# The first two weight tiles behind a sub-layer border: 258-column products of both tiles ahead of the 256-column ones

## The chip, the cores and the metric

The kernel runs as one program on 1 core of one Trainium2 chip. The metric is device time in microseconds (us) of one execution; lower is better. Three runs of the kernel before gave 945.15, 945.64 and 947.23 us, median 945.64 us.

## The reference

Two decoder layers over 256 tokens and 1024 features, all in float32. Each layer is FFN, token mixer, FFN; the mixer is stick-breaking attention in layer 0 and a gated linear recurrence (RG-LRU) in layer 1. Every sub-layer first normalises its input and modulates it with a shift, a scale and a gate that come from a conditioning vector:

```python
def sublayer_input(x, g, mod_j):
    shift, scale, gate = mod_j[:, 0], mod_j[:, 1], mod_j[:, 2]
    h = rmsnorm(x, g) * (1 + scale[:, None, :]) + shift[:, None, :]
    return h, (1 + gate)[:, None, :]
...
for layer in range(DEPTH):
    h, g = sublayer_input(x, norm_g[layer, 0], mod[:, 0])
    x = x + MACARON_W * g * swiglu(h, ffn_w_gu[layer, 0], ffn_w_down[layer, 0])
    h, g = sublayer_input(x, norm_g[layer, 1], mod[:, 1])
    if layer % N_MIXERS == 0:
        y = stick_breaking_attention(h, sb_w_qkv[j], sb_w_o[j])
    else:
        y = rglru_block(h, lru_w_in[j], lru_conv_w[j], lru_conv_b[j], lru_w_r[j], lru_b_r[j],
                        lru_w_i[j], lru_b_i[j], lru_lambda[j], lru_w_out[j])
    x = x + g * y
    h, g = sublayer_input(x, norm_g[layer, 2], mod[:, 2])
    x = x + MACARON_W * g * swiglu(h, ffn_w_gu[layer, 1], ffn_w_down[layer, 1])
return rmsnorm(x, final_norm_g)
```

So there are six sub-layers, and five borders between one sub-layer and the next.

## The kernel before, in words

The activations lie transposed: a chunk is 128 features (partitions) by T = 256 tokens (columns), eight chunks (KD) make one activation. A weight tile is 128 output features of two kinds (two halves, `g` = 0 and 1, of 128 columns each) by eight chunks of input features.

**Three products for one.** A float32 product is made from three products in the type fp32r. Weights and activations are each split into a high part, rounded to fp32r, and a low part, what the rounding left. `group` (the matmul stands in line 615) issues for each chunk and half up to three passes: pass 0 is high weight by high activation (`wh` by `xh`), pass 1 is high weight by low activation (`wh` by `xl`), pass 2 is low weight by high activation (`wl` by `xh`). For a weight tile that is 8 chunks x 2 halves x 3 passes = 48 products of 128 x 128 weights by 256 columns. ScalarE (ACT) writes the high weight parts (line 585), VectorE (DVE) the low ones (line 588), in two pieces of 1024 columns for each tile.

**Rings of buffers.** `wh` and `wl` hold seven such pieces each. `hx` holds 20 activation parts, with a pitch of 320 columns; `hk` holds two more. In the built program the ring `hx` begins at byte 102720 of a partition and its pitch is 1280 bytes, so that all its buffers begin 64 bytes behind a multiple of 256; the two buffers of `hk` begin at bytes 128384 and 129408, 128 behind a multiple of 256, and all pieces of `wh` and `wl`, when they are loaded as weights, also 128 behind one. `hk` holds a copy of chunk 0, high and low (line 763 and `other_copy`), that some of the tiles behind a border use in place of the one in `hx` (`up` with `kick=True`): the six products of chunk 0 then read their columns from `hk`, and the next ones from `hx` again.

**A border.** The last step of a sub-layer (`down`) adds its output to `x` chunk by chunk (line 794). At once `scaled` writes the scaled but not yet normalised chunk, high on ACT and low on DVE (line 730), and ACT copies two columns behind the high part (the shift, high and low), so that it has TX = 258 columns. The first two weight tiles (NFIRST) of the next sub-layer are multiplied with these chunks in `up_first`, and the norm is applied to their results afterwards: 256 columns are scaled with the norm's factor, and columns 257 and 258 are what the shift adds. Of the three passes, 0 and 2 have 258 columns and pass 1 has 256. Between these products TensorE adds up the squares over the partitions (`rstd`, line 705, two products with the weights `none`); ACT makes the norm's factor of the sum, and then DVE and ACT write the normalised chunks (`norm`, lines 738, 557 and 746) for all further tiles. Two tiles take 96 products, and `rstd` two.

**What sets the order.** `Program.schedule` orders all instructions by a planner's cost table while the program is built: TensorE's products mostly as written, ACT's and DVE's by how late the planner thinks they may be. `rstd` is written ahead of the 37th product of the first border (the one to attention) and ahead of the 49th of the others.

The five borders lead to attention, to the second FFN, to layer 1's first FFN, to the RG-LRU and to the last FFN, in this order.

Of the kernel before, what the change touches and what calls it, by code (L numbers as in the profile page):

```python
# [10 lines left out]
AF = mybir.ActivationFunctionType  # L11
ALU = mybir.AluOpType
PSUM = bass.MemoryType.PSUM

P = 128
T = 256
TX = T + 2
D = 1024
KD = D // P
# [11 lines left out]
HALF = 1024  # L31
SQ = 8
NFIRST = 2
LAT0, RATE0, RATE = 1250.0, 404.0, 360.0
LAT1 = 1250.0
LASTY = 900.0
# [357 lines left out]
def c_act(n, psum=False, ptr=0):  # L394
    return (51.0 if psum else 93.0) + 0.8333 * n + 93.0 * ptr


def c_dve(n):
    return 68.0 + 1.042 * n


def c_mm(n, passes=3):
    return (432.0 if passes == 4 else 114.0 * passes) * max(n, 256) / 256
# [7 lines left out]
def trunk(ctx, tc, first_in, cb, par, modw, gu, wdn, qk, wv, wo, win, wri, wout, out):  # L411
# [5 lines left out]
    act, dve, pe, pool, sp = nc.scalar, nc.vector, nc.tensor, nc.gpsimd, nc.sync  # L417
# [6 lines left out]
    def f32(ap):  # L424
        return ap.bitcast(F32)


    def ring(name, n, cols, dt=F32, pl=const, pitch=0):
        if pitch:
            whole = pl.tile([P, n * pitch], dt, tag=name, name=name)  # L430
            tiles = [whole[:, i * pitch : i * pitch + cols] for i in range(n)]
        else:
            tiles = [pl.tile([P, cols], dt, tag=f"{name}{i}", name=f"{name}{i}") for i in range(n)]
        return Space(name, n, lambda at, _: tiles[at]), tiles

    banks, _ = ring("bank", 8, 512, pl=psum)
    banks.exclusive = True
    rawr, _ = ring("raw", 3, CH)
# [14 lines left out]
    hxr, _ = ring("hx", 20, TX, F32R, pitch=320)  # L453
    const.tile([P, HKPAD], F32, tag="pad2", name="pad2")
    hkr, _ = ring("hk", 2, T, F32R)
    sqr, _ = ring("sq", 2, T)
    ssqr, _ = ring("ssq", 2, T)
    rmsr, _ = ring("rms", 1, T)
    rstr, _ = ring("rst", 1, T)
    hpr, _ = ring("hpre", 3, T)  # L460
    bcr, _ = ring("bc", 4, 2)
    tr, _ = ring("tr", 2, T)
    sgr, _ = ring("sg", 3, T)
# [36 lines left out]
    def fixed(name, cols, dt=F32):  # L500
        return const.tile([P, cols], dt, tag=name, name=name)
# [17 lines left out]
    none_ = fixed("none", P, F32R)  # L519
# [35 lines left out]
    def A(o, i, f, n, r, w, table=None, psum=False, ptr=0, after=(), **kw):  # L555
        def fn():
            act.activation(o(), i(), f, **{k: (v() if callable(v) else v) for k, v in kw.items()})  # L557
        return pr.op("ACT", c_act(n, psum, ptr), fn, r, w, after, table)

    def V(fn, n, r, w, cost=None, ptr=0, after=()):  # L560
        return pr.op("DVE", cost or c_dve(n) + 62.0 * ptr, fn, r, w, after)
# [33 lines left out]
    class Acc:  # L595
# [6 lines left out]
        def group(self, part, o, w, wc, xs, xc, stop, parts=(None,), passes=(0, 1, 2), m=None):  # L602

            b = self.b
            start = not self.started
            self.started = True
            wh, wl = w
            xh, xl = xs

            def fn():  # L610
                seq = ((wh, xh), (wh, xl), (wl, xh))
                for n, i in enumerate(passes):
                    u, v = seq[i]
                    c = slice(0, m if i == 1 else None)
                    pe.matmul(o(b())[:, c], wc(u()), xc(v())[:, c], start=start and n == 0,  # L615
                              stop=stop and n == len(passes) - 1, skip_group_check=True)

            n = xs_n[0]
            ws = [wh] * (passes != (2,)) + [wl] * (2 in passes)
            rd = ws + [(xh, q) for q in parts if passes != (1,)] + [(xl, q) for q in parts[:1] if 1 in passes]  # L620
            if not start:
                rd.append((b, "start"))
            wr = [(b, part)] + ([(b, "start")] if start else [])
            return pr.op("PE", c_mm(n, len(passes)), fn, rd, wr)
# [68 lines left out]
    def rstd(gen):  # L693
        qs = ssq.pop(gen)
        b = Buf(banks)
        sign = 1.0
        if not isinstance(qs, tuple):

            t, y, sign = qs, (Buf(hkr), Buf(hkr)), -1.0
            A(y[0], t, AF.Copy, T, [t], [y[0]])  # L700
            V(lambda: dve.tensor_tensor(y[1](), t(), f32(y[0]()), ALU.subtract), T, [t, y[0]], [y[1]])

            def fn():
                for i in range(2):
                    pe.matmul(b()[:, :T], none_, y[i](), start=i == 0, stop=i == 1)  # L705
            pr.op("PE", c_mm(T, 2), fn, list(y), [b])
            qs = ()
        for i, q in enumerate(qs):
            if gen == (0, 0):
                (q, c, h), o = q, slice(0, T)  # L710
            else:
                q, c, h, o = (q[0], q[2], q[1], q[2]) if isinstance(q, tuple) else (q, slice(0, T), None, slice(0, T))
            pr.op("PE", 259.2 if gen == (0, 0) else c_mm(T, 4), lambda i=i, q=q, c=c, o=o: pe.matmul(
                b()[:, o], ones, q()[:, c], start=i == 0, stop=i == len(qs) - 1, skip_group_check=True),
                [(q, h)] + [b] * (i > 0), [b])
        r = Buf(rmsr)
        o = Buf(rstr)
        A(r, lambda: b()[:, :T], AF.Ln, T, [b], [r], table="lnexp", psum=True, ptr=1, bias=eps_t, scale=sign / D)
        A(o, r, AF.Exp, T, [r], [o], table="lnexp", scale=-0.5)
        return o  # L720

    def scaled(gen, d):

        gs, y = mfin[gen + (1,)], shr[gen]
        hi, lo = Buf(hxr), Buf(hxr)
        gcur.setdefault(gen, []).append((hi, lo))
        c = slice(d, d + 1)
        A(lambda: hi()[:, T:], lambda: f32(y()[:, 2 * d : 2 * d + 2]), AF.Copy, 2, [(y, 0), (y, 1)], [(hi, 1)])
        A(lambda: hi()[:, :T], x[d], AF.Copy, T, [x[d], (gs, d)], [(hi, 0)], ptr=1, scale=lambda: gs()[:, c])
        V(lambda: dve.scalar_tensor_tensor(lo()[:, :T], x[d](), gs()[:, c], f32(hi()[:, :T]), ALU.mult, ALU.subtract), T,  # L730
          [x[d], (gs, d), (hi, 0)], [(lo, 0)], ptr=1)
# [19 lines left out]
    def norm(gen, q):  # L751
        for d in range(KD):
            norm_chunk(gen, d, q)
        other_copy(gen)
# [95 lines left out]
    def up_first(gen, ws, scale=(1.0, 1.0)):  # L850


        gx = gcur.pop(gen)
        accs = {}
        for i, w in enumerate(ws):
            accs[i] = [Acc(f"first_{gen}_{i}_{g}") for g in range(2)]
            for k in range(KD):
                if (i, k) == ((0, 6) if gen == (0, 1) else (1, 0)):
                    q = rstd(gen)
                for g in range(2):  # L860
                    c0 = (k % 4) * 256 + g * P
                    group(accs[i][g], 0, lambda b: b[:, :TX], w[k // 4], lambda u, c0=c0: u[:, c0 : c0 + P], gx[k],
                          lambda v: v, TX, k == KD - 1, parts=(0, 1), m=T)

        def evict(i, g):
            b, t, c = accs[i][g].b, Buf(tr), Buf(bcr)
            V(lambda: dve.tensor_scalar(c()[:, :1], b()[:, T : T + 1], b()[:, T + 1 : TX], scale[g], ALU.add, ALU.mult), 1, [b], [c],
              ptr=1, after=[lows[gen]])
            V(lambda: dve.scalar_tensor_tensor(t(), b()[:, :T], scale[g], q(), ALU.mult, ALU.mult), T, [b, q], [t],
              after=[lows[gen]])  # L870
            return t, c, lambda: c()[:, :1]

        norm(gen, q)
        for i in range(len(ws)):
            yield [evict(i, g) for g in range(2)]
# [13 lines left out]
    def ffn(l, s, nxt, hook):  # L889
# [12 lines left out]
        if j == 0:  # L902
            f0 = SQ
            accs = [Acc(f"g0_{f}") for f in range(SQ)]
            first_loads(F)
            q = rstd((0, 0))

            gb, goff, boff = gbias, OFF_NG, OFF_MB
# [92 lines left out]
        else:  # L1001
            f0 = NFIRST

# [17 lines left out]
    def attention(l, s, nxt, hook):  # L1021
# [43 lines left out]
        def q_load(f):  # L1065
            return load(qk[f], CH, f"qk{f}")

        def q_proj(f):
            if f == 0:
                firsts.append(up_first((l, s), [q_load(i) for i in range(NFIRST)], (0.125, 1.0)))  # L1070
            y = qs[f] = Buf(F, 4, name=f"q{f}")
# [4 lines left out]

            if f < NFIRST:
                for g, (t, rd, c) in enumerate(next(firsts[0])):
# [155 lines left out]
    def rglru(l, s, nxt):  # L1234
# [63 lines left out]
        def xb_proj(n2):  # L1298
            if n2 == 0:
                firsts.append(up_first((l, s), [  # L1300
                    load(win[1, i], CH, f"xb{i}", homes=ahead[1, 0] if i == 0 else ()) for i in range(NFIRST)]))
            if n2 < NFIRST:
                ts = next(firsts[0])
# [200 lines left out]
    parts = [(0, 0, 2), (0, 1, 1), (0, 1, 0), (0, 1, 2), (0, 2, 1), (0, 2, 0), (0, 2, 2)]  # L1504
# [96 lines left out]
```

## Time and profile before

| | us |
|---|---|
| median of 3 runs | 945.64 |
| span of the profiled execution | 943.5 |
| PE busy in it | 934.2 |
| DVE busy in it | 780.0 |
| ACT busy in it | 558.3 |
| first border, its 98 products | 193.03 to 204.67 |
| second border | 302.67 to 314.31 |

The profile is that of one execution, on the one core; its span runs from the first to the last instruction, and the median of the runs is 2.1 us above it. Matmuls overlap: a matmul's duration in the profile is longer than the distance from its start to the next one's, so that the pace of TensorE is read from the starts in the timeline, which prints them to 0.01 us, and the count of products between two of them. In the timeline neighbouring instructions of one group share a row, with the start of the first and their number; a product with 256 columns and one with 258 share a row where their tiles are the same.

### The profile page before, as it was taken

The numbers are of one execution on the slowest core, as the hardware profiler recorded it, in microseconds if no ns is written. First come the engines' busy times: TensorE is split into PE (matmuls) and PEld (weight loads), VectorE is DVE, ScalarE is ACT, GpSimd is POOL, SyncE is SP. The second block draws the span as 40 slices with busy tenths as digits, with TensorE's granted clock in tenths as the row PEclk, the third lists the DMA queues.
The fourth block names the chain that finished last, engine by engine and source line by source line (L and its number), as shares of the span: only waits on it lengthen the run. The fifth ranks groups of instructions, "written<-read, shape, count | busy, mean of one in ns | idle before, by whom it ended". The sixth has DMA issues, their size and how long they took to land.

```text
span 943.5 us, 19620 instructions
## 1 busy us (share of the span) xinstructions
PE 934.2 (99%) x8092; PEld 925.7 (98%) x8092; DVE 780.0 (83%) x1247; ACT 558.3 (59%) x921; POOL 2.1 (0%) x14
## 2 busy tenths in 40 slices
PE   8999999999999999999999999999999999999997
PEld 7999999999999999999999999999999999999997
DVE  8999988899978998888899998866999997555444
ACT  6785453488776754454376544535789685544333
POOL 0000000000000000000000000000000000000000
PEclk9999999999999999999999999999999999999999
DMA  9989899958752888889967999886333656555531
GB/s 365 404 335 365 323 345 356 347 207 299 275 202 96 309 335 324 311 328 349 361 263 275 353 336 334 326 332 224 135 129 141 224 184 242 199 184 203 167 118 45
DMA packets 48489, 251.24 MB, mean 266 GB/s; under 512 B 5384, under 2 KB 6288, under 8 KB 28688
## 3 DMA queue, kind: packets, MB, share of 16 engines
q1 hardware_dynamic: 48096, 249.59, 71.2%
q8 instruction: 63, 1.03, 0.4%
q10 hardware_dynamic: 304, 0.40, 0.1%
q14 instruction: 26, 0.21, 0.1%
HBM read 248.92 MB, written 1.05 MB: 265 GB/s over the span
## 4 chain that ended last, share of the span: by engine, by line
PE 95%; DMA 3%; DVE 1%; ACT 0%; SPq 0%; issue 0%; DVEq 0%; ACTq 0%
PE bank L615 89%; DMA raw<-in_first_in 3%; PE bank L1052 2%; PE bank L1285 1%; DMA arenar<-in_first_in 1%; PE bank L1118 1%; PE bank L1179 1%; PE bank L1155 1%; SPq L550 0%; DVE wl L588 0%; ACT wh L585 0%; DVE raw L1416 0%; PE bank L1158 0%; PE bank L1399 0%; PE bank L705 0%; DVE arenar L649 0%
## 5 line engine op out<-in xcount | busy, mean ns | idle before, releaser
L615 PE MATMUL bank<-hx,wh 128*128 128x256 f32 (+1 forms) x3264 | 559.7, 277 | 0.0
L585 ACT ACTIVATE wh<-raw 128x1024 fp32r<-128x1024 f32 (+1 forms) x330 | 336.8, 1038 | 292.7 <-PE bank L615 215.7
L615 PEld LDWEIGHTS bank<-hx,wh 128*128 128x128 f32 x3264 | 493.2, 188 | 0.3 <-DVE hx L951 0.2
L588 DVE TENSOR_TENSOR wl<-raw,wh 128x1024 fp32r<-128x1024 f32 (+1 forms) x330 | 387.7, 1195 | 122.7 <-ACT wh L585 118.7
L615 PE MATMUL bank<-hx,wl 128*128 128x256 f32 (+1 forms) x1640 | 452.5, 277 | 0.2 <-DVE wl L588 0.2
L615 PEld LDWEIGHTS bank<-hx,wl 128*128 128x128 f32 x1640 | 308.1, 188 | 0.4 <-DVE wl L588 0.4
L615 PE MATMUL bank<-arenar,wh 128*128 128x256 f32 x1696 | 289.4, 276 | 0.0
L615 PEld LDWEIGHTS bank<-arenar,wh 128*128 128x128 f32 x1696 | 255.6, 188 | 0.3 <-issue 0.3
L615 PE MATMUL bank<-arenar,wl 128*128 128x256 f32 x848 | 234.2, 276 | 0.0
L649 DVE SCALAR_TENSOR_TENSOR rawm<-rawm,cact 128x1024 f32<-128x1024 f32 x128 | 154.5, 1218 | 7.1 <-DMA rawm<-in_modw 6.8
L615 PEld LDWEIGHTS bank<-arenar,wl 128*128 128x128 f32 x848 | 159.2, 188 | 0.1
L557 ACT ACTIVATE arenar<-a 128x256 fp32r<-128x256 f32 x88 | 35.1, 403 | 7.2 <-DVE a L882 7.1
L887 DVE TENSOR_TENSOR arenar<-a,arenar 128x256 fp32r<-128x256 f32 x88 | 36.2, 417 | 0.5 <-ACT arenar L557 0.5
L882 DVE TENSOR_TENSOR a<-bank,sg 128x256 f32<-128x256 f32 x82 | 34.0, 417 | 0.6 <-ACT sg L557 0.4
L557 ACT ACTIVATE sg<-bank 128x256 f32<-128x256 f32 x82 | 29.8, 367 | 6.7 <-PE bank L615 6.6
L557 ACT ACTIVATE arenaf<-bank 128x256 f32<-128x256 f32 (+1 forms) x53 | 22.8, 486 | 11.9 <-DVE bank L1128 4.5
L794 DVE SCALAR_TENSOR_TENSOR x<-bank,mf,x 128x256 f32<-128x256 f32 (+1 forms) x49 | 21.7, 471 | 9.2 <-PE bank L615 9.1
L557 ACT ACTIVATE hx<-x,mf 128x256 fp32r<-128x256 f32 x40 | 19.1, 499 | 15.7 <-DVE x L794 15.7
L557 ACT ACTIVATE hx<-hpre,mf 128x256 fp32r<-128x256 f32 x41 | 19.9, 500 | 8.7 <-DVE hpre L738 8.6
L1052 PE MATMUL bank<-wh,hx 128*128 128x256 f32 x128 | 23.5, 281 | 0.0
L649 DVE SCALAR_TENSOR_TENSOR arenar<-arenar,cact 128x1024 f32<-128x1024 f32 x16 | 19.4, 1218 | 1.0 <-DMA arenar<-in_first_in 0.9
L1052 PEld LDWEIGHTS bank<-wh,hx 128*128 128x128 f32 x128 | 20.1, 189 | 0.1
(126 smaller groups left out, 504.3 us busy)
## 6 DMA issues: line engine op xcount, KB each, us to landing
raw<-in_gu SPq DMA_DIRECT2D x79, 1024.0 KB, 4.9
rawm<-in_modw SPq DMA_DIRECT2D x128, 512.0 KB, 6.6
raw<-in_wdn SPq DMA_DIRECT2D x44, 1024.0 KB, 5.1
raw<-in_win SPq DMA_DIRECT2D x10, 1024.0 KB, 4.8
arenar<-in_first_in SPq DMA_DIRECT2D x16, 512.0 KB, 8.0
raw<-in_qk SPq DMA_DIRECT2D x8, 1024.0 KB, 5.1
raw<-in_wout SPq DMA_DIRECT2D x5, 1024.0 KB, 5.0
raw<-in_first_in SPq DMA_DIRECT2D x8, 512.0 KB, 8.8
```

Source lines behind the costliest of these rows:

```text
L557: act.activation(o(), i(), f, **{k: (v() if callable(v) else v) for k, v in kw.items()})
L585: act.activation(h()[:, :m], raw()[:, a : a + m], AF.Copy)
L588: dve.tensor_tensor(lo()[:, :m], raw()[:, a : a + m], f32(h()[:, :m]), ALU.subtract)
L615: pe.matmul(o(b())[:, c], wc(u()), xc(v())[:, c], start=start and n == 0, stop=stop and n == len(passes) - 1, skip_group_check=True)
L649: dve.scalar_tensor_tensor(raw(), raw(), 1.0, cact(), ALU.mult, ALU.mult, accum_out=m()[:, t : t + 1])
L794: dve.scalar_tensor_tensor(x[d]()[:, w], acc.b()[:, j * T + w.start : j * T + w.stop], gate()[:, d : d + 1], x[d]()[:, w], ALU.mult, ALU.add)
L882: V(lambda: dve.tensor_tensor(a(), b()[:, T:], sg(), ALU.mult), T, [(b, (1, 0)), sg], [a])
L887: V(lambda: dve.tensor_tensor(y[1](), a(), f32(y[0]()), ALU.subtract), n, [a, y[0]], [y[1]])
L1052: pe.matmul(o, u()[:, tb * P : (tb + 1) * P], v()[:, c0 : c0 + 256], start=start and n == 0, stop=k == KD - 1 and n == 2, skip_group_check ...
L1118: pe.matmul(zb[e][i]()[:, j * m : (j + 1) * m], y()[rows, kc], y()[rows, qc], start=j == 0, stop=j == 1, skip_group_check=True)
L1155: pe.matmul(b()[:, : NC[i]], ntri, blk(q(), i), start=False, stop=i == j == 1, skip_group_check=True)
L1179: pe.matmul(b()[e * 64 : (e + 1) * 64, j * T + tb * P : (j + 1) * T], v()[:, vc : vc + 64], ww[e]()[:, at : at + NC[tb] // 2], start=j == ...
```

## The change

Three things, all in what belongs to a border:

- In `up_first` the order of the 96 products is another one. First come the passes 0 and 2 (258 columns) of tile 0, chunk by chunk, then those of tile 1: 64 products. Then come the passes 1 (256 columns): for each chunk those of tile 0 and of tile 1, 32 products. `rstd` is written ahead of chunk 1 of tile 1 at the first border and ahead of chunk 4 of tile 1 at the others.
- In `scaled` the low parts of chunks 0 and 1 (KICKS) are written to the ring `hk` in place of `hx`. These are the columns of the first 8 of the 32 products of pass 1.
- In `rstd` the two parts of the sum of squares are written to `hx` in place of `hk`.

```diff
+KICKS = 2
...
-            t, y, sign = qs, (Buf(hkr), Buf(hkr)), -1.0
-            A(y[0], t, AF.Copy, T, [t], [y[0]])
-            V(lambda: dve.tensor_tensor(y[1](), t(), f32(y[0]()), ALU.subtract), T, [t, y[0]], [y[1]])
+            t, y, sign = qs, (Buf(hxr), Buf(hxr)), -1.0
+            h, m = lambda: y[0]()[:, :T], lambda: y[1]()[:, :T]
+            A(h, t, AF.Copy, T, [t], [y[0]])
+            V(lambda: dve.tensor_tensor(m(), t(), f32(h()), ALU.subtract), T, [t, y[0]], [y[1]])
...
-                    pe.matmul(b()[:, :T], none_, y[i](), start=i == 0, stop=i == 1)
+                    pe.matmul(b()[:, :T], none_, y[i]()[:, :T], start=i == 0, stop=i == 1)
...
-        hi, lo = Buf(hxr), Buf(hxr)
+        hi, lo = Buf(hxr), Buf(hkr if d < KICKS else hxr)
...
-        accs = {}
-        for i, w in enumerate(ws):
-            accs[i] = [Acc(f"first_{gen}_{i}_{g}") for g in range(2)]
+        accs = [[Acc(f"first_{gen}_{i}_{g}") for g in range(2)] for i in range(len(ws))]
+
+        def products(i, k, passes):
+            for g in range(2):
+                c0 = (k % 4) * 256 + g * P
+                group(accs[i][g], 0, lambda b: b[:, :TX], ws[i][k // 4], lambda u, c0=c0: u[:, c0 : c0 + P], gx[k], lambda v: v,
+                      TX, k == KD - 1 and passes == (1,), parts=(0, 1), passes=passes, m=T)
+
+        for i in range(len(ws)):
             for k in range(KD):
-                if (i, k) == ((0, 6) if gen == (0, 1) else (1, 0)):
+                if (i, k) == ((1, 1) if gen == (0, 1) else (1, 4)):
                     q = rstd(gen)
-                for g in range(2):
-                    c0 = (k % 4) * 256 + g * P
-                    group(accs[i][g], 0, lambda b: b[:, :TX], w[k // 4], lambda u, c0=c0: u[:, c0 : c0 + P], gx[k],
-                          lambda v: v, TX, k == KD - 1, parts=(0, 1), m=T)
+                products(i, k, (0, 2))
+        for k in range(KD):
+            for i in range(len(ws)):
+                products(i, k, (1,))
```

TensorE's order at the second border, its first products, as the kernel before has it. `bank` are the accumulators, `hx` the activation parts, `wh` and `wl` the weight parts (the number behind a name is the buffer); the last column is what the columns' operand is, partitions by columns.

```order
1738 L615 MATMUL bank_67<-arenar_2524,wl_90 128x256
1739 L615 MATMUL bank_65<-hx,wh_84 128x258
1740 L615 MATMUL bank_65<-hx,wh_84 128x256
1741 L615 MATMUL bank_65<-hx,wl_91 128x258
1742 L615 MATMUL bank_70<-hx,wh_84 128x258
1743 L615 MATMUL bank_70<-hx,wh_84 128x256
1744 L615 MATMUL bank_70<-hx,wl_91 128x258
```

The same place with the change; `group`'s matmul is line 616 of the changed file.

```order
1738 L616 MATMUL bank_67<-arenar_2540,wl_90 128x256
1739 L616 MATMUL bank_63<-hx,wh_84 128x258
1740 L616 MATMUL bank_63<-hx,wl_91 128x258
1741 L616 MATMUL bank_70<-hx,wh_84 128x258
1742 L616 MATMUL bank_70<-hx,wl_91 128x258
```

The products with 256 columns have left this place. They stand at the end of the border, opened by eight that read from `hk`:

```order
1803 L616 MATMUL bank_69<-hx,wl_87 128x258
1804 L616 MATMUL bank_63<-hk_95,wh_84 128x256
1805 L616 MATMUL bank_70<-hk_95,wh_84 128x256
1806 L616 MATMUL bank_68<-hk_95,wh_79 128x256
1807 L616 MATMUL bank_69<-hk_95,wh_79 128x256
1808 L616 MATMUL bank_63<-hk_96,wh_84 128x256
1809 L616 MATMUL bank_70<-hk_96,wh_84 128x256
1810 L616 MATMUL bank_68<-hk_96,wh_79 128x256
1811 L616 MATMUL bank_69<-hk_96,wh_79 128x256
1812 L616 MATMUL bank_63<-hx,wh_84 128x256
```

In the kernel before, no product of the border reads `hk` but the two of `rstd`; behind these rows 23 more from `hx` follow, all with `wh`, and then the first tile of the normalised chunks.

ACT's order at the first border, before: `hx<-x` is a scaled high part, `hx<-sh` the two columns of the shift, `wh<-raw` a weight piece of a later tile, `hk<-ssq` the sum of squares for `rstd`.

```order
184 L557 ACTIVATE sq_97<-x 128x256
185 L557 ACTIVATE hx<-sh_186 128x2
186 L557 ACTIVATE hx<-x,mf_158 128x256
187 L557 ACTIVATE lam<-x 128x10
188 L557 ACTIVATE hk_95<-ssq_99 128x256
189 L557 ACTIVATE hx<-sh_186 128x2
190 L585 ACTIVATE wh_84<-raw_73 128x1024
191 L557 ACTIVATE hx<-sh_186 128x2
192 L585 ACTIVATE wh_78<-raw_73 128x1024
```

And with the change:

```order
183 L558 ACTIVATE sq_97<-x 128x256
184 L558 ACTIVATE hx<-x,mf_158 128x256
185 L558 ACTIVATE hx<-sh_186 128x2
186 L586 ACTIVATE wh_84<-raw_73 128x1024
187 L558 ACTIVATE hx<-sh_186 128x2
188 L586 ACTIVATE wh_78<-raw_73 128x1024
189 L558 ACTIVATE hx<-ssq_99 128x256
```

The sum of squares for `rstd` now stands behind these two weight pieces, where it stood ahead of both; the last copy of the shift stands behind one weight piece in either order.

## Prediction

> **What bounds the kernel now.** First the page: the busy times, the clock, the chain that ended last.
>
> ```profile
> span 943.5 us, 19620 instructions
> PE 934.2 (99%) x8092; PEld 925.7 (98%) x8092; DVE 780.0 (83%) x1247; ACT 558.3 (59%) x921; POOL 2.1 (0%) x14
> ...
> PEclk9999999999999999999999999999999999999999
> ...
> PE 95%; DMA 3%; DVE 1%; ACT 0%; SPq 0%; issue 0%; DVEq 0%; ACTq 0%
> ```
>
> TensorE is 95% of the chain and the granted clock is full in all slices. Next, the waits of TensorE:
>
> ```profile
> PE bank L927 <- DVE hpre L743: 1.2, 1, 1.2
> PE bank L1446 <- POOL eps L511: 1.2, 1, 1.2
> PE bank L615 <- DVE wl L588: 0.2, 1, 0.2
> ```
>
> That is 2.6 us in all, none at a border. So a change inside a border can win only by letting TensorE issue the same products at a shorter distance, and lose by making it wait or by lengthening that distance. Hence the timeline, for the distance from start to start. A long stretch behind the second border (groups, then its first and last rows; the row at 423.16 is the first product of the next kind):
>
> ```profile
> L615 PE MATMUL bank<-hx,wh 128*128 128x256 f32 x636 | 108.2, 276 | 0.0
> L615 PE MATMUL bank<-hx,wl 128*128 128x256 f32 x318 | 87.8, 276 | 0.0
> ```
>
> ```profile
> 314.31 0.40 PE L615 MATMUL bank<-hk,wh 128*128 128x256 f32 x2
> ...
> 315.02 0.40 PE L615 MATMUL bank<-hx,wh 128*128 128x256 f32 x2
> ...
> 315.72 0.39 PE L615 MATMUL bank<-hx,wh 128*128 128x256 f32 x2
> ...
> 423.16 0.39 PE L615 MATMUL bank<-arenar,wh 128*128 128x256 f32 x2
> ```
>
> 636 + 318 = 954 products from 315.02 on; the first six take 0.70 us (117 ns each), the other 948 take 107.44 us: **113.3 ns** each. The six from `hk` ahead of them take 0.71 us, 118 ns each. I call 113.3 ns the settled pace. Not every stretch of the same shape has it. Behind the first border, from 204.67 to 216.06:
>
> ```profile
> L1052 PE MATMUL bank<-wh,hx 128*128 128x256 f32 x32 | 6.0, 280 | 0.0
> L615 PE MATMUL bank<-hx,wh 128*128 128x256 f32 x28 | 5.0, 281 | 0.0
> L1052 PE MATMUL bank<-wl,hx 128*128 128x256 f32 x16 | 4.5, 280 | 0.0
> L615 PE MATMUL bank<-hx,wl 128*128 128x256 f32 x14 | 3.9, 281 | 0.0
> L615 PE MATMUL bank<-hk,wh 128*128 128x256 f32 x4 | 0.8, 282 | 0.0
> L615 PE MATMUL bank<-hk,wl 128*128 128x256 f32 x2 | 0.6, 283 | 0.0
> ```
>
> ```profile
> 204.67 0.28 PE L1052 MATMUL bank<-wh,hx 128*128 128x256 f32 x1
> ...
> 209.62 0.40 PE L615 MATMUL bank<-hk,wh 128*128 128x256 f32 x2
> ...
> 216.06 0.49 PE L1118 MATMUL bank<-arenaf 64*128 64x256 f32 x2
> ```
>
> The first 42 products (to 209.62: 48 of L1052 less the six that stand behind the six of `hk`) take 4.95 us, **117.9 ns** each, the unsettled pace; all 96 take 11.39 us, 118.6 ns each. Same columns, same clock, no wait: the pace has a memory, and what stood ahead decides. Now the second border itself:
>
> ```profile
> L615 PE MATMUL bank<-hx,wh 128*128 128x256 f32 x32 | 9.1, 283 | 0.0
> L615 PE MATMUL bank<-hx,wl 128*128 128x258 f32 x32 | 9.0, 282 | 0.0
> L615 PE MATMUL bank<-hx,wh 128*128 128x258 f32 x32 | 9.0, 280 | 0.0
> ```
>
> ```profile
> 302.67 0.40 PE L615 MATMUL bank<-hx,wh 128*128 128x258 f32 x2
> 302.90 0.28 PE L615 MATMUL bank<-hx,wl 128*128 128x258 f32 x1
> 303.02 0.41 PE L615 MATMUL bank<-hx,wh 128*128 128x258 f32 x2
> ```
>
> It ends at 314.31: these 96 and `rstd`'s two, 98 products in 11.64 us, 118.8 ns each. At the settled pace they would take 11.11 us; so five borders hold at most 5 x 0.53 = 2.7 us, 0.28% of the time. Of that the change can win a part. About 0.2% is what a measurement of this kernel can tell from no change, here 1.9 us.
>
> **The change, part by part.** (1) *The 64 products with 258 columns, now in one row.* No such row exists in the trace. Bounds: the settled pace by columns, 113.3 x 258/256 = 114.2 ns; and 120 ns, the distance of single 258-column products (302.90 to 303.02). I take 117.9 ns, the unsettled pace at 256 columns: TensorE comes to the border from settled products, and the third one in it already takes 0.12 us, so a row with the wider ones more likely stays unsettled than not. 64 x 0.1179 = 7.55 us. (2) *`rstd`'s two*, at 0.12 us 0.24 us, before and after. (3) *The eight from `hk`*: 8 x 0.118 = 0.94 us. (4) *The 24 with 256 columns behind them.* In the rows at 314.31 six products from `hk` came straight out of a border, and then `hx` needed six (0.70 us) to settle. Here eight come out of 258-column products in the same way: 0.70 + 18 x 0.1133 = 2.74 us. If they don't settle: 24 x 0.1179 = 2.83 us.
>
> One border is then 7.55 + 0.24 + 0.94 + 2.74 = 11.47 us, against 11.64: 0.17 us won, **0.85 us in five**. With 114.2 ns for (1) it is 0.41 us and 2.04 us; with 120 ns 0.04 us and 0.2 us; not settling in (4) takes back 5 x 0.09 = 0.45 us.
>
> The rule that speaks against it: the Trainium skill, "TensorE: Matmul & The Clock Gate", section "Wait — 56ns, not 53.3ns?", gives a stream's distance as the columns over 2.4 GHz plus some 2.5 ns that are fixed per matmul, so by it order and address cost nothing and the sum would be 0. The trace disagrees, with 113.3 and 117.9 ns for the same 256 columns.
>
> (5) *Behind the first border* no copy of chunk 0 opens the next tile, and the 96 products above ran unsettled. Left in the settled pace they would save 96 x (118.6 - 113.3) = 0.5 us; but they read other operands at once and change them more often than before, so I take half, **0.25 us**, with bounds of 0 and 0.5. At the other four a tile opened from `hk` follows at once, before and after, which settles the pace from either side; from a settled stretch as here:
>
> ```profile
> 62.42 0.39 PE L615 MATMUL bank<-hk,wh 128*128 128x256 f32 x2
> ...
> 63.13 0.40 PE L615 MATMUL bank<-hx,wh 128*128 128x256 f32 x2
> ...
> 63.83 0.39 PE L615 MATMUL bank<-hx,wh 128*128 128x256 f32 x2
> ```
>
> Again 0.71 us and 0.70 us: nothing won or lost there.
>
> (6) *What TensorE now needs earlier.* The last high chunk is needed after 28 to 30 products instead of 36 to 42, and the weights of tile 1 after 32 instead of 48. At the first border, the tightest, ACT has:
>
> ```profile
> 194.98 0.49 ACT L557 ACTIVATE hx<-x,mf 128x256 fp32r<-128x256 f32 x1
> 195.38 0.20 ACT L557 ACTIVATE lam<-x 128x10 f32<-128x10 f32 x1
> 195.48 0.41 ACT L557 ACTIVATE hk<-ssq 128x256 fp32r<-128x256 f32 x1
> 195.80 0.19 ACT L557 ACTIVATE hx<-sh 128x2 fp32r<-128x2 f32 x1
> 195.89 1.04 ACT L585 ACTIVATE wh<-raw 128x1024 fp32r<-128x1024 f32 x1
> 196.84 0.19 ACT L557 ACTIVATE hx<-sh 128x2 fp32r<-128x2 f32 x1
> ```
>
> ```profile
> 195.92 0.43 DVE L701 TENSOR_TENSOR hk<-ssq,hk 128x256 fp32r<-128x256 f32 x1
> ```
>
> In the new order the last high chunk (194.98, 0.40 to the next start) is followed by a shift (0.09), a weight piece (0.95), the last shift (0.19): ready at 196.61. TensorE comes to it after 30 products, 193.03 + 30 x 0.1179 = 196.57. Then another piece (0.95, from 196.51), and the sum of squares from 197.46: ACT 0.41, DVE 0.43, ready at 198.30; TensorE wants it after 44 products, at 198.22. So both arrive on the brink: **0.15 us lost**, bounds 0 and 0.4. The other four have `rstd` four products later and no such squeeze. (7) *The low parts of chunks 0 and 1 in `hk`* keep the copy of chunk 0 waiting until their products are done, after 70 and 74 products, at 310.92 and 311.39 at the second border. There the two copies start later anyway, so it costs nothing:
>
> ```profile
> 311.19 0.42 ACT L557 ACTIVATE hk<-hx 128x256 fp32r<-128x256 f32 x1
> ```
>
> ```profile
> 311.90 0.29 DVE L763 CAST hk<-hx 128x256 fp32r<-128x256 f32 x1
> ```
>
> DMAs, bytes and the number of instructions stay; no queue is passed by a DMA.
>
> **Sum:** -0.85 - 0.25 + 0.15 = -0.95 us: the profiled execution from 943.5 to 942.5 us, and the median, 2.1 us above it, from 945.64 to **944.7 us**.
>
> **The rivals.**
> - *A row of 258-column products settles* at 114.2 ns. For it: in settled stretches all products of a row have one width, and the border mixes two. Against: at the border's entry the settled pace is lost within three products. 2.04 + 0.25 - 0.15 = 2.1 us won, 943.5 us.
> - *Nothing settles:* the row runs at 120 ns, and the last 24 stay at 117.9. -0.2 + 0.45 + 0.15 = +0.4 us, 946.0 us; with only one of the two, about 945.5 us. For it: eight from `hk`, all with `wh`, is not the pattern of six that the trace shows settling.
> - *The distance depends on the columns alone*: 945.6 us. By the skill's page this is the outcome; with two paces in the rows it has little.
> - *Slower:* the six from `hk` behind a border no longer settle the 948 products after them, because they now come out of another state. One such stretch costs 948 x (117.9 - 113.3) = 4.4 us, so that a single one of the four borders decides: 945.64 - 0.95 + 4.4 = 949.1 us. Against it: rows 314.31 and 62.42 settle from both states.
>
> **How the numbers follow.** Forecast (row of 258 unsettled, 256 settled) 0.50; the row settles 0.22; nothing settles 0.16; columns alone 0.05; slower 0.07. Faster by over 1.9 us needs the row to settle, three in four of these cases (943.5 is only just beyond), 0.165, and a tenth of the forecast's: 0.22. Slower: 0.07. Between: 0.71. The range goes from a settled row with all of (5), 945.64 - 2.4 = 943.2, to 946.0, where nothing settles.
>
> **What would show it.** Right: in the timeline of a border 64 products with 258 columns take 7.4 to 7.7 us, the last 18 with 256 columns 2.04 us, and TensorE has no wait of over 0.4 us there. Wrong: 7.3 us for the 64 (settled, and the gain is double), 0.1179 us each at the end (no settling), a stretch of 948 that lasts 111.8 in place of 107.4 us, or waits for the sum of squares, a shift or a normalised low part at several borders.

## The result, and the profile after

| | median, us | lowest to highest | executions |
|---|---|---|---|
| before | 945.91 | 945.15 to 953.63 | 20 |
| changed | 952.01 | 945.66 to 952.72 | 20 |

The ratio is 1.0048, with a 95% interval of 1.0036 to 1.0061: slower by some 0.5%, where I had forecast 944.7 us and had put the upper end at 946.0. The executions of the changed kernel fall into two groups, which the medians hide: 5 of the 20 lie at 945.7 to 946.9, as before, and 15 at 951.9 to 952.7. I call the second group the long executions. With the later runs below they are 20 of 33; of the kernel before they are 6 of 103.

The profile that came with the result is of a short one (span 944.6, device time 946.28 us). Its page: busy times and the chain as before.

```profile
span 944.6 us, 19604 instructions
PE 934.9 (99%) x8092; PEld 926.3 (98%) x8092; DVE 780.0 (83%) x1247; ACT 558.6 (59%) x921; POOL 2.1 (0%) x14
...
PE 95%; DMA 4%; DVE 0%; ACT 0%; issue 0%; SPq 0%; DVEq 0%; ACTq 0%
```

TensorE's longest waits, of which none is at a border:

```profile
PE bank L935 <- DVE hpre L745: 1.4, 1, 1.4
PE bank L1454 <- POOL eps L512: 1.2, 1, 1.2
```

The second border and the stretch behind it in TensorE's timeline (start, duration, operation, count):

```profile
303.27 0.28 PE L616 MATMUL bank<-hx,wh 128*128 128x258 f32 x1
...
309.07 0.40 PE L707 MATMUL bank<-hx,none 128*128 128x256 f32 x2
309.31 0.28 PE L616 MATMUL bank<-hx,wh 128*128 128x258 f32 x1
...
311.24 0.64 PE L616 MATMUL bank<-hk,wh 128*128 128x256 f32 x4
...
312.20 0.41 PE L616 MATMUL bank<-hx,wh 128*128 128x256 f32 x2
...
314.94 0.39 PE L616 MATMUL bank<-hk,wh 128*128 128x256 f32 x2
...
315.65 0.40 PE L616 MATMUL bank<-hx,wh 128*128 128x256 f32 x2
...
423.84 0.39 PE L616 MATMUL bank<-arenar,wh 128*128 128x256 f32 x2
```

The 64 wide products take 5.80 + 1.93 = 7.73 us, 120.8 ns each; `rstd` 0.24; the eight from `hk` 0.96; the 24 behind them 2.74: together 11.67 us, against 11.64 before. Then six from `hk` in 0.71 and 954 products in 108.19 us, 113.4 each with the first six. So in a short execution the border wins nothing and the stretch is settled. The first border:

```profile
193.64 0.28 PE L616 MATMUL bank<-hx,wh 128*128 128x258 f32 x1
...
205.31 0.28 PE L1060 MATMUL bank<-wh,hx 128*128 128x256 f32 x1
...
216.66 0.49 PE L1126 MATMUL bank<-arenaf 64*128 64x256 f32 x2
```

11.67 us again (before 11.64), and 11.35 us for the 96 products behind it (before 11.39). It begins 0.6 us later than before, which comes from the start of the kernel: in two later profiles of the same program it begins at 194.11 (look_1) and 192.97 us (look_2).

### The profile page after: what moved, and what is told of

The parts are those of the page before. It is cut to its first block, busy times and chain, and to the rows that moved or that the text cites. A ratio compares the mean times of both kernels' runs of the same rounds, so it can differ in the third digit from the quotient of the medians.

```text
span 944.6 us, 19604 instructions
## 1 busy us (share of the span) xinstructions
PE 934.9 (99%) x8092; PEld 926.3 (98%) x8092; DVE 780.0 (83%) x1247; ACT 558.6 (59%) x921; POOL 2.1 (0%) x14
## 4 chain that ended last, share of the span: by engine, by line
PE 95%; DMA 4%; DVE 0%; ACT 0%; issue 0%; SPq 0%; DVEq 0%; ACTq 0%
PE bank L616 89%; DMA raw<-in_first_in 3%; PE bank L1060 2%; PE bank L1293 1%; DMA arenar<-in_first_in 1%; PE bank L1126 1%; PE bank L1187 1%; PE bank L1163 1%; DMA x<-in_first_in 0%; DVE raw L1424 0%; PE bank L1166 0%; PE bank L1407 0%; DVE wl L589 0%; PE bank L707 0%; ACT wh L586 0%
## 5 line engine op out<-in xcount | busy, mean ns | idle before, releaser
L616 PE MATMUL bank<-hx,wl 128*128 128x256 f32 (+1 forms) x1640 | 447.2, 277 | 0.1
L748 DVE SCALAR_TENSOR_TENSOR hx<-hpre,mf,hx 128x256 fp32r<-128x256 f32 x41 | 19.1, 479 | 1.5 <-ACT hx L558 1.4
```

The costliest lines, as they stand in the source:

```text
L748: V(lambda: dve.scalar_tensor_tensor(lo()[:, :T], hp(), sh()[:, c], f32(hi()[:, :T]), ALU.add, ALU.subtract), T, [hp, (sh, d), hi], [lo], ...
```

## The experiments

**1. The same program again.** same_1 and same_2 are the changed kernel, for the spread and for more profiles.

> The changed kernel once more, to have a profile of one of its long executions (15 of its 20 runs took 951.9 to 952.7 us, 5 took 945.7 to 946.9 us; the profile of it that is there belongs to one of 946.3 us, in which every long stretch runs at the settled 113.3 ns). Theory A, a stretch behind a border loses its pace: in a profile of about 950.5 us span one or more of the long stretches runs at 117.8 ns; 6.2 us over 4.44 ns are 1395 products, so most of one FFN behind its border, 954 + 528 products, is unsettled, and TensorE has no new wait. Theory B, waits: TensorE waits some 6 us more, for normalised low parts or weights at several borders. Theory C, the start: the 6 us lie in the first 193 us, before the first border, and the change only moved the start's luck.

> The changed kernel a second time, for a second profile: with 15 long executions in 20 the chance that neither of two profiles is long is 1 in 16. Theory A: if both are long, it is the same stretch in both. Theory B: the waits differ a little. Theory C: the lost time lies in the first 193 us.

same_1: 946.18 us median of 10 (945.54 to 953.29), four of them long; before 945.57 (13 executions, two long); ratio 1.0018, interval 0.9986 to 1.0049. same_2: 945.73. Both profiles were of short executions, so that nothing yet told where the 6 us go.

**2. Without the low parts in `hk`.** `KICKS = 2` becomes `KICKS = 0`; the eight products that open the 256-column ones read from `hx`.

> The changed kernel with KICKS = 0: the low parts of chunks 0 and 1 stay in hx, so the 32 products of 256 columns follow the 64 of 258 with no eight from hk between. Theory A in the form that the eight from hk settle the 32: these 32 now run at 117.8 ns or worse (3.8 us instead of 3.7 a border, +0.1 us each), the border is left unsettled as in the kernel before, the following six from hk meet the same kind of state as there, and the long executions vanish: about 946.2 us in all runs. Theory B: the long executions stay, about 952 us. Theory C: the long executions stay.

956.93 us median of 4 (953.58 to 959.62), ratio 1.0125 (1.0092 to 1.0158): no short execution at all, the opposite of what I expected. The 32 products of pass 1 settled without the eight from `hk` at borders two to five, and the second border took 11.61 us, where the changed kernel takes 11.67. But in the profile, of the execution of 954.64 us, the stretch behind the second border ran unsettled, 954 and 528 products at 117.7 and 117.8 ns. It was the first profile that showed a lost stretch, though not why. Besides, TensorE waited there behind the third border, for low parts, some 1.2 us in all. The two executions at 959.2 and 959.6 us have no profile.

**3. A long execution of the changed kernel, and three tests of what stands around the border.** look_1 and look_2 are the changed kernel; in no_copy_behind the FFNs behind a border don't read the copy; rings_alone has before's order of products with the change's rings.

```diff
-            up(acc, load(...), (l, s), f == (f0 + 1 if j == 0 else f0))
+            up(acc, load(...), (l, s), j == 0 and f == f0 + 1)
```

> The changed kernel once more, for one execution's profile. Theory A (in a long execution one stretch of 1,482 products behind one border never gets back to the settled pace): if this execution is a long one (about 952 us, two in three so far), exactly one stretch of 954 + 528 products runs at 117.7 to 117.8 ns in place of 113.3, which is 6.5 us, and the others are as in the short ones; if it is a short one (about 946 us), none. Rival B (in a long execution TensorE waits somewhere): a wait of several us stands in the waits and all stretches are settled. Rival C (the start of the kernel differs): the first border begins 6 us later.

> As look_1, the changed kernel again: a long execution has exactly one stretch of 1,482 products at 117.7 to 117.8 ns (Theory A), or a wait of several us (B), or a first border 6 us later (C).

> The changed kernel with the first tile of the three FFNs behind a border reading chunk 0 from hx and not from its copy in hk (the copies are still written); the RG-LRU and the attention keep theirs. Theory A1 (the six products from hk are what unsettles a stretch that comes out of the border settled): no execution is long behind these three borders, so nearly all are at 945 to 946.5 us. Theory A2 (the border's end settles or not by chance, and the six from hk mostly mend it): without them long executions are at least as common, and some have two lost stretches, 952 and 958.5 us. Rival B (waits): no difference to the changed kernel, about two in three executions at 952 us.

> Before's order of the 96 products of a border, with the ring moves of the change alone: the low parts of chunks 0 and 1 in hk and the sum of squares in hx. Theory A (the new order of products, with its row of 64 wide ones, puts TensorE into the state from which a stretch is lost): as before, 945 to 946 us, long executions no more frequent than before's 3 in 33. Rival D (where the low parts of chunks 0 and 1 and the sum of squares lie is what costs the stretch): long executions in a third of the runs or more.

look_1 was a long one, 953.19 us; look_2 a short one, 945.57. In look_1 the first border begins at 194.11, no wait of TensorE at a border stands in the list, and one stretch is lost, as Theory A said. The granted clock has no part in it: 0.996 in look_1, and 0.996 as well in the short execution of sum_early below; the profiles of long executions have 0.996 to 0.999, those of short ones too. But the stretch isn't lost at the border. Its timeline (its span is 951.5 us):

```profile
315.41 0.39 PE L616 MATMUL bank<-hk,wh 128*128 128x256 f32 x2
...
318.85 0.39 PE L616 MATMUL bank<-hx,wh 128*128 128x256 f32 x2
319.08 0.28 PE L616 MATMUL bank<-hx,wl 128*128 128x256 f32 x1
319.19 0.45 PE L616 MATMUL bank<-hx,wh 128*128 128x256 f32 x2
319.47 0.28 PE L616 MATMUL bank<-hx,wl 128*128 128x256 f32 x1
319.59 0.40 PE L616 MATMUL bank<-hx,wh 128*128 128x256 f32 x2
319.83 0.28 PE L616 MATMUL bank<-hx,wl 128*128 128x256 f32 x1
...
428.42 0.40 PE L616 MATMUL bank<-arenar,wh 128*128 128x256 f32 x2
...
490.61 0.28 PE L616 MATMUL bank<-hx,wh 128*128 128x258 f32 x1
```

Read the distances by triples. From 318.85 to 319.19, three products, is 0.34 us: settled. From 319.19 to 319.47, two products, is 0.28 us where 0.23 is due: 0.05 us too long, at the 35th product behind the border. I call such a long distance a stumble. From 319.47 to 319.83, three products, is 0.36 us: unsettled, and so it stays for 925 products to 428.42 (108.95 us, 117.8 each) and for 528 more to the third border (62.19 us, 117.8 each; the group of those with `wh` in this window has 352, and half as many have `wl`):

```profile
L616 PE MATMUL bank<-arenar,wh 128*128 128x256 f32 x352 | 62.2, 281 | 0.0
```

The short execution has the same stumble at the same product, and there the settled pace survives (from 319.00 to 319.35, three products, 0.35 us, and 0.34 for the triples that follow):

```profile
318.73 0.44 PE L616 MATMUL bank<-hx,wh 128*128 128x256 f32 x2
319.00 0.28 PE L616 MATMUL bank<-hx,wl 128*128 128x256 f32 x1
319.12 0.39 PE L616 MATMUL bank<-hx,wh 128*128 128x256 f32 x2
319.35 0.28 PE L616 MATMUL bank<-hx,wl 128*128 128x256 f32 x1
...
483.68 0.28 PE L616 MATMUL bank<-hx,wh 128*128 128x258 f32 x1
```

From the stumble to the third border it takes 164.68 us, look_1 171.14 for the same 1,453 products: 6.46 us, as much as the two groups lie apart. What is late is read on DVE. Before, behind the second border (`hpre` is the normed chunk, `hx` its low part, `wl` a weight piece of a later tile):

```profile
310.14 1.26 DVE L738 SCALAR_TENSOR_TENSOR hpre<-x,mf,rst 128x256 f32<-128x256 f32 x3
...
313.30 1.22 DVE L588 TENSOR_TENSOR wl<-raw,wh 128x1024 fp32r<-128x1024 f32 x1
...
316.81 0.88 DVE L746 SCALAR_TENSOR_TENSOR hx<-hpre,mf,hx 128x256 fp32r<-128x256 f32 x2
```

And with the change, in the short execution:

```profile
310.74 1.27 DVE L740 SCALAR_TENSOR_TENSOR hpre<-x,mf,rst 128x256 f32<-128x256 f32 x3
...
314.20 1.23 DVE L589 TENSOR_TENSOR wl<-raw,wh 128x1024 fp32r<-128x1024 f32 x1
...
315.74 1.22 DVE L589 TENSOR_TENSOR wl<-raw,wh 128x1024 fp32r<-128x1024 f32 x1
...
318.25 0.48 DVE L748 SCALAR_TENSOR_TENSOR hx<-hpre,mf,hx 128x256 fp32r<-128x256 f32 x1
```

The norm begins 7.47 us behind the border's first product in both. But from there to the low part of the sixth chunk, which product 35 is the first to read, DVE now writes two weight pieces where it wrote one, so that this low part ends at 318.73, 0.11 us ahead of the start of its product (the second of the row at 318.73). In the kernel before, the low part of the sixth chunk is the first of the two at 316.81. There product 32 reads it first, the second of the row

```profile
317.76 0.39 PE L615 MATMUL bank<-hx,wh 128*128 128x256 f32 x2
```

and it starts 0.58 us behind the end of that write; product 35 reads the same low part again, 0.92 us behind it. (The expectation of late_sum_before below takes these 0.58 and 0.92 us for two low parts. They are one, and the spare time is the 0.58.) In the profiles without the stumble no low part behind the second border comes less than 0.35 us ahead.

no_copy_behind: 949.52 us median of 10, five long, ratio 1.0034 (1.0008 to 1.0060), so A1 (the copy is to blame) fell. Behind the third and the fifth border its tiles run at 113.3 ns without the six from `hk`. Its profile is of a long one, and has a larger stumble at the same product, 0.32 us for two:

```profile
318.33 0.48 PE L616 MATMUL bank<-hx,wh 128*128 128x256 f32 x2
318.65 0.28 PE L616 MATMUL bank<-hx,wl 128*128 128x256 f32 x1
```

rings_alone: 945.92 us (945.47 to 948.09, 11 executions, none long), ratio 1.0004 (0.9995 to 1.0013). There that low part comes 0.65 us ahead of its first product, the 32nd, and no distance is too long. So the rings alone don't make long executions. They aren't free: its second border takes 11.72 us in place of 11.64, too little for the median to show. It is with the new order of products that the planner writes that weight piece earlier. no_hk_rows has the stumble too:

```profile
319.63 0.44 PE L616 MATMUL bank<-hx,wh 128*128 128x256 f32 x2
319.91 0.28 PE L616 MATMUL bank<-hx,wl 128*128 128x256 f32 x1
```

**4. Theory W: one wait of 0.05 us for a low part.** Three kernels: the second tile opened from `hk` as well; the sum of squares of the second border four products earlier; and the kernel before with its sum of squares there 12 products later. Of each changed line the part that differs:

```diff
-(l, s), f == (f0 + 1 if j == 0 else f0))
+(l, s), f == f0 + 1 or j > 0 and f == f0)
...
-((1, 1) if gen == (0, 1) else (1, 4))
+((1, 1) if gen == (0, 1) else (1, 3) if gen == (0, 2) else (1, 4))
...
-((0, 6) if gen == (0, 1) else (1, 0))
+((0, 6) if gen == (0, 1) else (1, 2) if gen == (0, 2) else (1, 0))
```

> The changed kernel, and the second tile of an FFN behind a border reads chunk 0 from the copy in hk too. Theory W (behind the second border one product waits some 0.05 us for the low part of a normalised chunk, 34 products behind the border; that wait throws TensorE off the settled pace in about two of three executions, and nothing resettles it for the rest of the 1,482 products): the wait stays, but the second tile, at most 48 products later, settles the pace again, so that the loss is at most 48 x 4.4 ns = 0.2 us, and all executions lie at 945.5 to 947 us. Rival K (the copy in hk itself, read by a tile that comes out of the border, is what throws it off): long executions at 952 us stay at least as frequent.

> The changed kernel with the sum of squares of the second border written four products earlier, ahead of chunk 3 of tile 1. Theory W: the normalised low parts behind the second border come up to 0.45 us earlier, the product that waited has some 0.4 us to spare, no distance there is over 130 ns, and the long executions go: all at 945.5 to 947 us. Rival R (the row of 64 wide products, or the border's end, leaves TensorE in a state that later falls out of the settled pace by itself): long executions as frequent as before, two in three. If the planner or the sum of squares itself (ready at 309.0, wanted then at about 309.05) eats the 0.45 us, the wait and the long executions stay, and that tells nothing against W.

> The kernel before, its order of products and its rings kept, with the sum of squares of the second border alone written 12 products later (1.4 us). In the kernel before, the low part that the 35th product behind this border reads is ready 0.92 us ahead, and the one three products earlier 0.58 us. Theory W: both come too late now, TensorE waits behind the border for some 0.1 to 0.8 us in all, and many executions lose the settled pace of that stretch: long ones at 952 to 953 us in a third of the runs or more, the others at 945.6 to 946.5. Rival R (it takes the change's order of products): no long executions beyond before's few, and only the wait itself is lost, 0.1 to 0.8 us.

sum_early: 946.10 us (945.61 to 947.30), none long of 11, ratio 1.0006 (0.9997 to 1.0015). The stumble is gone: the nearest low part comes 0.36 us ahead, and the stretch runs at 113.3. This is Theory W's outcome. The changed kernel wasn't run again beside it. Of what was, second_kick, which has the stumble, is long in six of 9, and the kernel before in none of 26.

second_kick: 952.07 us, six long of 9, ratio 1.0053 (1.0031 to 1.0074). It tests less than I thought: the planner lays the first two tiles side by side, and the second tile's six from `hk` come ahead of product 35. What its profile, of a long one, does show is how little a stumble needs to be. Here two products take 0.24 us where 0.23 is due, and the pace is lost:

```profile
318.03 0.40 PE L616 MATMUL bank<-hx,wh 128*128 128x256 f32 x2
318.27 0.28 PE L616 MATMUL bank<-hx,wl 128*128 128x256 f32 x1
```

late_sum_before: 945.83 us, one long of 12, ratio 1.0009 (0.9996 to 1.0021). No wait came about: the planner moved DVE's steps along, and the low part still came 0.76 us ahead. It tells nothing of W.

**5. The wait made, the loss mended, the wide row by itself.** third_kick opens the third tile behind a border from `hk` too. late_low_before is the kernel before, where one low part is written three times; TensorE, ACT and the rest of DVE keep their order. narrow_row leaves out most of the shift: of the 64 wide products only the first of each accumulator keeps 258 columns. Again the parts of lines that differ:

```diff
-(l, s), f == (f0 + 1 if j == 0 else f0))
+(l, s), f == f0 + 1 if j == 0 else f in (f0, f0 + 2))
...
+        def low():
+            for _ in range(3 if (gen, d) == ((0, 2), 5) else 1):
+                dve.scalar_tensor_tensor(lo()[:, :T], hp(), sh()[:, c], f32(hi()[:, :T]), ALU.add, ALU.subtract)
...
-                    c = slice(0, m if i == 1 else None)
+                    c = slice(0, m if i == 1 or not (start and n == 0) else None)
```

> The changed kernel, and the third tile of an FFN behind a border (its product 67 behind the second border, 32 behind the one that waits) reads chunk 0 from the copy in hk too. Theory W (one wait throws TensorE off the settled pace, and nothing puts it back): six products from hk put it back, so that a lost pace costs some 35 products x 4.4 ns = 0.15 us in place of 6.5, and all executions lie at 945.5 to 947 us. Rival K (six products from hk do not settle TensorE once a wait has thrown it off, or are themselves what throws it off): long executions at 952 us in half of the runs or more, as in the changed kernel.

> The kernel before, in its own order on every engine, but behind the second border DVE writes the low part of the sixth normalised chunk three times over (twice for nothing, 0.8 us). The product that reads it had 0.58 us to spare. Theory W: it waits some 0.25 us now, and a third or more of the executions lose the settled pace there: long ones at 952 to 953 us, the others at 945.5 to 946.5. Rival R (the lost pace takes the border's new order of products): no long executions beyond before's few (4 in 80 so far), 945.8 us.

> The changed kernel with 256 columns in place of 258 in the 64 wide products of a border, but for the first of each accumulator: it leaves out the shift of chunks 1 to 7. Theory N (the two columns more set the pace of the row: 120.8 ns each in the changed kernel): the 60 products settle at 113.3 ns or run at 117.8. Rival P (the row's pattern, two weights in turn on the same columns without a low part between, sets it): 120 to 121 ns at 256 columns too.

late_low_before: of 12 executions three at 959.1 to 959.4, one at 953.0, the others 945.8 to 947.5; median 947.27, ratio 1.0032 (0.9998 to 1.0065). So a wait alone does it, in before's order and rings, in 4 of 12; the kernel before is long in 2 of the 23 executions beside it and in 6 of 103 in all, and never above 953.7 us. Its profile is of one at 959.35. DVE's four writes (three of the sixth chunk's low part and one of the next chunk's), the stumble, and the third border's end:

```profile
317.24 1.91 DVE L749 SCALAR_TENSOR_TENSOR hx<-hpre,mf,hx 128x256 fp32r<-128x256 f32 x4
```

```profile
318.19 0.28 PE L615 MATMUL bank<-hx,wh 128*128 128x256 f32 x1
318.81 0.39 PE L615 MATMUL bank<-hx,wh 128*128 128x256 f32 x1 [0.35 <-DVE hx L749]
...
502.17 0.40 PE L615 MATMUL bank<-hk,wh 128*128 128x256 f32 x2
...
502.88 0.40 PE L615 MATMUL bank<-hx,wh 128*128 128x256 f32 x2
...
615.24 0.40 PE L615 MATMUL bank<-arenar,wh 128*128 128x256 f32 x2
```

The wait is 0.62 - 0.11 = 0.51 us (the two repeated writes end 1.04 us behind the first one, and not 0.8), and the stretch is lost. What I hadn't expected is the second loss: TensorE comes to the third border unsettled, the six from `hk` at 502.17 don't settle it, and 954 products take 112.36 us, 117.8 each. Two stretches make 13 us.

third_kick: 946.38 us (945.65 to 947.63), none long of 12, against 20 of 33 without it; ratio 1.0007 (0.9995 to 1.0019). The changed kernel wasn't run again beside it. The third tile begins at product 97 behind the border in its profile, 62 behind the stumble, and not at 67 as I had counted. The stumble is still there, 0.29 us for two:

```profile
319.52 0.45 PE L616 MATMUL bank<-hx,wh 128*128 128x256 f32 x2
319.81 0.28 PE L616 MATMUL bank<-hx,wl 128*128 128x256 f32 x1
```

Within five products the pace was back in the profiled execution, long before the six from `hk`, so that the mending itself isn't seen in a trace; that no execution is long is what speaks for it, and it isn't shown.

narrow_row: 946.10 us, one execution. Its wide row, now with 256 columns, at the second border (28 products lie from the first row to the second; the last is the first from `hk` behind the border, which begins at 304.47):

```profile
304.47 0.28 PE L616 MATMUL bank<-hx,wh 128*128 128x258 f32 x1
...
304.94 0.28 PE L616 MATMUL bank<-hx,wh 128*128 128x256 f32 x1
...
308.11 0.28 PE L616 MATMUL bank<-hx,wh 128*128 128x258 f32 x1
...
315.77 0.39 PE L616 MATMUL bank<-hk,wh 128*128 128x256 f32 x2
```

3.17 us for 28, 113.2 ns each: settled, in the same pattern of operands. Only the 16 behind `rstd` run at 117.8. So the two columns cost the row 7.6 ns a product, and the border takes 11.30 in place of 11.67 us. At the first border TensorE then comes too early for ACT, for the sum of squares above all, and that border takes 12.95 us.

## Why the prediction was wrong

**The step that failed** is in part (5): at the other four borders "a tile opened from `hk` follows at once, before and after, which settles the pace from either side", and so "nothing won or lost there". The tile is followed by the settled pace, in look_1 too. But I took the settled pace as something that then lasts. A single stumble can end it, and part (6) looked for a stumble only inside the borders and only where tens of nanoseconds count as nothing: "The other four have `rstd` four products later and no such squeeze." I followed the engines up to the border's end and did not read DVE's order behind it, where one weight piece more stands ahead of a low part. In look_1 a wait of 0.05 us for that low part costs 6.46 us.

**The rival that ended slower** had the size of it: "a single one of the four borders decides", 4.4 us for a stretch of 948. The measured loss is larger by the 528 products of the sub-layer's last step, which I had left out of the stretch. Its mechanism was another (that the six from `hk` fail because of where they come from), so that it came near for the wrong reason, and its chance of 0.07 was argued from the wrong rows: those at 314.31 and 62.42 show two entries from which six settle, and late_low_before shows one from which they don't. "Settles from either side" was more than two rows could carry.

**(1) The wide row** was mis-sized as well: 120.8 ns and not 117.9, above my upper bound of 120. That is 64 x 2.9 = 0.19 us a border, 0.93 in five, and takes all of the 0.85 us that I forecast. The bound came from a single distance in a mixed row. By an estimate from the Trainium skill, "TensorE: Matmul & The Clock Gate", section "Wait — 56ns, not 53.3ns?", two columns more would cost 2 / 2.4 = 0.8 ns. The traces disagree, with 7.6 ns between narrow_row and the changed kernel.

**(2), (3), (4)** held: `rstd` 0.24, the eight 0.96 against 0.94, the 24 2.74 as forecast. But no_hk_rows settled there without the eight, so that my reason for (4) was not needed: the 2.74 us don't bear it out. **(5) at the first border** gave 0.04 us and not 0.25: the 24 products that follow, which have `wh` and `wl` as their columns, run at 118.0 ns though they come out of settled ones. **(6)** cost nothing, because the slow row gave ACT time; narrow_row, with a faster row, waits there as part (6) had feared, and its first border takes 1.6 us more than its second. **(7)** held: behind the second border the copy is written 2.2 us ahead of the products that read it.

**What stays open:** why the same stumble loses the pace in some executions and not in others. In the profiles, stumbles of 0.01 (second_kick), 0.05 (look_1, no_hk_rows), 0.09 (no_copy_behind) and 0.51 us (late_low_before) lost it, and ones of 0.05 (the result's profile, look_2) and 0.06 us (same_1, same_2, third_kick, narrow_row) did not. Nor does a longer wait always lose it. In no_hk_rows, behind the third border, the product at 506.28 starts 0.50 us behind the one before it, some 0.39 us late. From 507.32 to 508.34, nine products, is 1.02 us, which is settled, and behind some more such waits the rest of that stretch runs at 113.3 ns:

```profile
506.28 0.39 PE L616 MATMUL bank<-hx,wh 128*128 128x256 f32 x1 [0.16 <-DVE hx L748]
...
507.32 0.39 PE L616 MATMUL bank<-hx,wh 128*128 128x256 f32 x2
...
508.34 0.39 PE L616 MATMUL bank<-hx,wh 128*128 128x256 f32 x2
```

So the runs show that the wait makes long executions frequent, and not what decides in the single one. Also open is where the 6 long executions of the kernel before lose theirs: none was profiled.

## What to carry to other kernels

When a trace shows two paces for the same instructions, find out what ends the fast one as well as what begins it, and price each wait by the stretch behind it and not by its length. Behind a changed stage read the order of the engines that feed the next one, since a planner may move their steps too. And where runs fall into two groups, profile one of each: a profile of the fast group shows the stumble here, but not what it costs the median.

## What the runs showed of the hardware that I had not expected

- A wait of TensorE of 0.05 us can cost 6.46 us (look_1): it leaves the pace of 113.3 ns for 117.8, and 1,453 products of 256 columns without another pause don't bring it back. In the result's profile a wait of the same length costs itself alone.
- The list of waits doesn't show such a wait. The distance of two products in the timeline does (0.28 for 0.23 us), and so does the mean duration of a group (281 in place of 276 ns).
- Rows of 258 columns run at 120.8 ns a product in the changed kernel, the same rows with 256 at 113.2 to 117.8.
- Behind a border, six products from `hk` are followed by the settled pace in most profiles, but not in each (502.17 in late_low_before). That the six are what settles it isn't shown: no_copy_behind has 113.3 ns without them behind the third and the fifth border.
